# Tail of a hybrid decoder layer on one core: pools opened ahead of the attention branch, conv states moved into w_down, final norm by token quarters

## The chip, the core and the metric

One NeuronCore of a Trainium2 chip. TensorE (PE) multiplies, VectorE (DVE), ScalarE (ACT) and GpSimd (POOL) do the elementwise work, SyncE (SP) issues transfers; ACT and POOL can issue transfers on queues of their own. Each engine runs its instructions in order. The metric is the time of one execution on the device in microseconds (us).

## What is computed

One step of a one-layer decoder trunk on 1024 prompt tokens and 8 x 4 sample tokens, 1056 columns in all, in float32:

```
x      (1024 prompt + 32 sample tokens) x 1024
attn   = dilated sliding-window attention      -> 256 channels
ssm    = diagonal state space, GELU, half-GLU  -> 512 channels
mix    = sigmoid(ga) * (attn @ w_branch_attn) + sigmoid(gs) * (ssm @ w_branch_ssm)
x      = x + mix @ w_out
g, v   = halves of rmsnorm(x) @ w_up           (2816 channels each)
h      = v * silu(causal width-3 convolution of g over the tokens)
x      = x + h @ w_down
y      = rmsnorm(x)                            outputs y_prompt, y_sample
conv_p, conv_s = the last two values of g of every sequence
```

The outputs conv_p and conv_s are the "conv states" below; the caches and state-space states that are also returned are written earlier.

## The kernel before, in words

**Layout.** Channels lie on partitions (1024 = 8 chunks of 128, 2816 = 22), tokens along the free axis: 1056 columns, either as 3 pieces of 352 or as 4 quarters of 264 (256 prompt and 8 sample columns each). A float32 product is made of three matmuls: each operand is split into a high part (a cast on ACT) and a low part (a subtraction on DVE). For weights that is `load_w`: load on SP (L156), cast (L157), subtraction (L158); for activations `split` (L187, L188). The order of the instructions on each engine is mostly set by a scheduler ahead of time, from the dependences and from when the buffers of the pools come free; program text sets it only roughly.

**From the branches to w_out.** The state-space branch leaves its gated product in DRAM (`msd`), the gate logits lie there too (`sgd`). Then x is turned: x_sample is loaded (L1283), blocks are transposed on PE and copied by ACT (L1299), and eight stores on SP (L1302) keep the result in DRAM as `xtd`, to be added after w_out. The attention branch runs over 8 row groups m and 3 column pieces, 24 chunks of 128 x 352 (L1320 to L1335): the gate is loaded into a `ck` buffer on SP (L1328), sigmoid on ACT (L1329), `msd` loaded on ACT's queue (L1331), multiplied with the product on DVE (L1332), added on POOL (L1333), and split into `mh`, `ml` (L187, L188). The pool `ck` has 6 buffers of each name. After the loop the pools `low`, which hold x, are closed, and `wb` (the pool of weights for w_out, w_up and the hidden loads) is opened. w_out (L176) takes all 8 `mh`, `ml` as its k; its first result is added to `xtd` by DVE (L1374).

**w_up** (`up(f)`, 22 blocks). Seven products a block, combined by DVE; ACT, DVE and POOL make the convolution (POOL's copies L1475 to L1477, ACT L1479, DVE L1480 and L1481), silu (ACT L1482), the gain (POOL L1483) and the product `gt` (DVE L1484), and SP stores it as rows of `hd` in DRAM (L1485). `cso` keeps the last columns of each sequence.

**Conv states** (L1490 to L1499). Six times: four transposes of `cso` on PE (L145), a copy on ACT into a `gt` buffer (L1496), four small stores on SP (L1498, L1499); 24 stores in all, of 1 to 16 KB.

**w_down and the final norm.** Four quarters q of 264 columns. `hidden(q)` loads the quarter's 22 row groups from `hd` in 11 pieces (L1519) and splits them. For each of 4 pairs of output rows m there are 6 weight tiles of up to 512 KB through `load_w`, 24 matmuls to a full tile (L1560), and DVE adds the residual `y` (L1563). `turned_half` transposes half of a 128-token block (4 matmuls, L145, and an ACT copy, L1534). `norm_out` does the final norm of one block: a square with its sum over 1024 columns on ACT (L1539), the reciprocal root in small steps (L250 to L256), one multiply over 1024 columns on DVE (L1541) and the store on SP (L1542). The 32 sample tokens are collected in `sy` and normed after the loop, in a buffer from the same pool as the others.

The order of the last lines is:

```
for q in range(S4):
    ...                       # w_down, turned halves
    for b in range(2):
        norm_out(2 * q + b, yT[b], P, ypv[q, b])
    G_.tensor_copy(sy[...], y[:, :, 256:])
    hs_ = nxt
ys = fb.tile(...)             # sample tokens
for q2 in range(2):
    turned_half(ys, q2, 32, lambda k: sy[:, k])
norm_out(8, ys, 32, O[1])
```

Of the kernel before, what the change touches and what calls it, by code (L numbers as in the profile page):

```python
# [18 lines left out]
P = 128  # L19
D = 1024  # L20
NB = 8
S4 = 4
C = 264
T = S4 * C
CH = 352
NCH = 3
KD = D // P
DFF = 2816
NF = DFF // P
# [70 lines left out]
def body(tc, I, O):  # L100
    nc = tc.nc
# [11 lines left out]
    with root:  # L113
# [29 lines left out]
        def tr(out, in_):  # L143
            n = in_.shape[0]
            PE.transpose(out, in_, ident[:n, :n])  # L145
# [1170 lines left out]
        for k in range(2):  # L1316
            split(ah[k], al[k], attnF[k])
        keep.close()
        psum(8)
        ck = pool("ck", 6, stack=s6a, side="right")  # L1320
        for m in range(KD):
            if m % 4 == 0:
                w = load_w(I['w_branch_attn'][0][:, m * P:(m + 4) * P], 2, mw=4 * P)
            ps = gbanks()
            gemm(ps, w, list(zip(ah, al)), m0=m % 4 * P)
            for c in range(NCH):
                t = ck.tile([P, CH], F32, name="ck")
                nc.sync.dma_start(t, sgd[0, m * P:(m + 1) * P, cs(c)])  # L1328
                A_.activation(t, t, AF.Sigmoid)  # L1329
                t2 = ck.tile([P, CH], F32, name="ck2")  # L1330
                nc.scalar.dma_start(t2, msd[m * P:(m + 1) * P, cs(c)])  # L1331
                V_.tensor_tensor(t, ps[c][:, :CH], t, OP.mult)  # L1332
                G_.tensor_tensor(t, t, t2, OP.add)  # L1333
                split(mh[m][:, cs(c)], ml[m][:, cs(c)], t)
        s6a.close()  # L1335
        low.close()

        NK = KD // 2  # L1340
        rb1 = pool("rbp", 1).tile([P, T], F32, name="rb1")
        xa = pool("xa", 1)
        wb = pool("wo", 2)
        XO = [None] * NK
        s6y = root.enter_context(ExitStack())
        yt_ = pool("yt", 1, stack=s6y)
# [49 lines left out]
        pu_ = pool("pu", 3, PSUM, stack=s7)  # L1396
        pe_ = pool("pe", 2, PSUM, stack=s7)

        cso = ff.tile([P, NF, 18], F32, name="cso")
        n9 = ff.tile([P, 3, 9], F32, name="n9")  # L1400
        blk9 = [(j, j * P, min(P, T - j * P)) for j in range(9)]
        pt = pe_.tile([P, 512], F32, name="pe")
# [34 lines left out]
        def up(f):  # L1437
# [44 lines left out]
            A_.activation(cv, cv, AF.Silu)  # L1482
            G_.tensor_tensor(cv, cv, rb2, OP.mult)  # L1483
            V_.tensor_tensor(gt, gt, cv, OP.mult)  # L1484
            nc.sync.dma_start(hd[f * P:(f + 1) * P], gt)  # L1485

        for f in range(NF):
            up(f)

        for f0 in range(0, NF, 4):  # L1490
            n = min(4, NF - f0)
            pt = pe_.tile([P, 512], F32, name="pe")
            for f in range(n):
                tr(pt[:18, f * P:(f + 1) * P], cso[:, f0 + f])
            co_ = ff.tile([P, T], F32, name="gt", bufs=2)[:18, :512]
            A_.copy(co_[:, :n * P], pt[:18, :n * P])  # L1496
            for i in range(2):
                nc.sync.dma_start(O[7][0, :, i, f0 * P:(f0 + n) * P], co_[9 * i:9 * i + 1, :n * P])  # L1498
                nc.sync.dma_start(O[13][0, :, i, f0 * P:(f0 + n) * P], co_[9 * i + 1:9 * i + 9, :n * P])  # L1499
        s7.close()  # L1500


# [27 lines left out]
        def turned_half(yT, q2, rows, cols):  # L1530
            pt = pt_.tile([P, 512], F32, name="pt")[:rows]
            for k in range(4):
                tr(pt[:, k * P:(k + 1) * P], cols(4 * q2 + k))
            A_.copy(yT[:, q2 * 512:(q2 + 1) * 512], pt)  # L1534

        def norm_out(b, yT, rows, dst):
            f = fr[:rows, b]
            yo = wb.tile([P, KD, P], F32, name="wlo").rearrange("p k m -> p (k m)")[:rows]
            A_.activation(yo, yT, AF.Square, accum_out=f[:, 0:1])  # L1539
            rsqrt(f[:, 1:2], f[:, 0:1], f[:, 2:3], V_)  # L1540
            V_.scalar_tensor_tensor(yo, yT, f[:, 1:2], gf[:rows], OP.mult, OP.mult)  # L1541
            nc.sync.dma_start(dst, yo)  # L1542

        hs_ = hidden(0)
        for q in range(S4):
            y = fb.tile([P, KD, C], F32, name="y")
            nc.sync.dma_start(y, yd2[:, q * C:(q + 1) * C].rearrange("(m p) c -> p m c", p=P))
            nxt = None
            yT = [wb.tile([P, KD, P], F32, name="whi").rearrange("p k m -> p (k m)") for _ in range(2)]
            for m in range(0, KD, 2):  # L1550
                ps = [pg.tile([P, 512], F32, name="pd") for _ in range(2)]
                for k0 in range(0, NF, 4):
# [8 lines left out]
                                          start=k0 + k == 0 and j == 0, stop=k0 + k == NF - 1 and j == 2)  # L1561
                for x in range(2):
                    V_.tensor_tensor(y[:, m + x], ps[x][:, :C], y[:, m + x], OP.add)  # L1563
                if m == 0 and q + 1 < S4:
                    nxt = hidden(q + 1)
                if m % 4 == 2:
                    for b in range(2):
                        turned_half(yT[b], m // 4, P, lambda k, b=b: y[:, k, b * P:(b + 1) * P])
            for b in range(2):
                norm_out(2 * q + b, yT[b], P, ypv[q, b])  # L1570
            G_.tensor_copy(sy.rearrange("p k (b s) -> p k b s", s=S4)[:, :, :, q], y[:, :, 256:])  # L1571
            hs_ = nxt
        ys = fb.tile([P, KD, C], F32, name="y").rearrange("p k c -> p (k c)")[:32, :D]
        for q2 in range(2):
            turned_half(ys, q2, 32, lambda k: sy[:, k])
        norm_out(8, ys, 32, O[1].rearrange("b t d -> (b t) d"))
        s9.close()


# [31 lines left out]
```

## Time and profile before

| | |
|---|---|
| three timed runs | 1714.08, 1715.98 (median), 1721.87 us |
| the profiled execution | 1716.02 us |
| its span in the profile | 1714.2 us |
| mean granted clock of TensorE | 0.967 |
| busy share of PE, DVE, ACT, POOL | 92%, 60%, 36%, 24% |
| data moved | 234.49 MB, 137 GB/s over the span |

The span begins with the first instruction that the profile shows and ends with the last; 1.8 us lie around it. Busy times leave out the issuing of transfers and waits. In the rows below "L156" is line 156 of the kernel, an arrow reads "out <- in", and "[13.63 <-DVE wlo L158]" says how long an engine had stood idle before a row and what ended it. A name with q (SPq, ACTq) is the queue of that engine: such a row is the issue of a transfer, not its flight. "x6" means six instructions of the same kind in a row, whose times are put together.

### The profile page before, as it was taken

How to read it: one execution, taken by the hardware profiler on the slowest of the kernel's cores; microseconds unless marked ns; L12 is line 12 of the kernel's file. 1: busy time of each engine (PE TensorE's matmuls, PEld its weight loads, DVE VectorE, ACT ScalarE, POOL GpSimd, SP SyncE). 2: the span in 40 equal slices, each digit the busy share in tenths (PEclk: the TensorE clock that was granted, in tenths of full speed). 3: DMA queues.
4: the chain of work that ended last, by engine and by line, in shares of the span. 5: the costliest groups of instructions: out<-in, count | busy, mean ns of one | idle time of the engine just before them, and what ended most of it. 6: DMA issues, size and time to landing. Idle time of an engine off the chain costs nothing. (4 is left out here: it accounts for less than half of the span.)

```text
span 1714.2 us, 28810 instructions
## 1 busy us (share of the span) xinstructions
PE 1576.7 (92%) x11523; PEld 1501.0 (88%) x11523; DVE 1026.5 (60%) x1681; ACT 619.6 (36%) x1113; POOL 406.4 (24%) x419
## 2 busy tenths in 40 slices
PE   6998978999999989997699999999999957999996
PEld 5898977988888878786699999999999947999996
DVE  6546988234444434334467888888888854556453
ACT  5211221234434433325345333333333334445342
POOL 0669364022212322403221111212111110000000
PEclk9999999999999999999899999999999978999998
DMA  8263311354345436676542222222222239678552
GB/s 226 69 172 129 102 51 50 102 151 136 86 117 142 124 99 247 194 268 233 175 151 88 63 76 81 81 75 76 75 81 82 76 118 285 213 259 267 178 194 80
DMA packets 272655, 234.49 MB, mean 137 GB/s; under 512 B 33269, under 2 KB 252895, under 8 KB 272522
## 3 DMA queue, kind: packets, MB, share of 16 engines
q1 hardware_dynamic: 258842, 210.75, 40.3%
q10 hardware_dynamic: 10352, 10.38, 1.9%
q0 software_dynamic: 3328, 11.54, 1.9%
q8 instruction: 90, 1.47, 0.4%
q14 instruction: 43, 0.35, 0.1%
HBM read 184.12 MB, written 50.46 MB: 137 GB/s over the span
## 5 line engine op out<-in xcount | busy, mean ns | idle before, releaser
L158 DVE TENSOR_TENSOR wlo<-wraw,whi 128x1024 fp32r<-128x1024 f32 (+1 forms) x148 | 182.7, 1235 | 166.2 <-ACT whi L157 160.5
L176 PE MATMUL pg<-xh,wlo 128*128 128x352 f32 x816 | 213.5, 343 | 4.1 <-ACT pt__5401 L872 2.7
L157 ACT CAST whi<-wraw 128x1024 fp32r<-128x1024 f32 (+1 forms) x148 | 148.2, 1003 | 173.6 <-PE pd L1560 114.9
L176 PE MATMUL pg<-xh,whi 128*128 128x352 f32 x816 | 199.8, 326 | 0.0
L176 PE MATMUL pg<-xl,whi 128*128 128x352 f32 x816 | 199.0, 325 | 0.0
L176 PEld LDWEIGHTS pg<-xh,wlo 128*128 128x128 f32 x816 | 142.4, 191 | 15.2 <-issue 5.6
L176 PEld LDWEIGHTS pg<-xh,whi 128*128 128x128 f32 x816 | 144.7, 190 | 0.0
L176 PEld LDWEIGHTS pg<-xl,whi 128*128 128x128 f32 x816 | 144.4, 191 | 0.3
L964 POOL TENSOR_TENSOR qb<-kt,qb 128x512 f32<-128x512 f32 x48 | 65.5, 1377 | 247.7 <-DMA qb<-qd 127.7
L187 ACT CAST sh<-S 128x512 fp32r<-128x512 f32 x88 | 52.2, 619 | 77.8 <-DVE S L1451 57.1
L1571 POOL COPY sy<-y 128x64 f32<-128x64 f32 x4 | 4.0, 997 | 293.7 <-DVE y L1563 293.7
L1483 POOL TENSOR_TENSOR cv<-cv,rb 128x1056 f32<-128x1056 f32 x22 | 54.4, 2472 | 70.0 <-ACT cv L1482 70.0
L1009 ACT COPY pTs<-pT 128x256 f32<-128x256 f32 (+1 forms) x48 | 22.6, 470 | 121.1 <-PE pT L145 119.2
L188 DVE TENSOR_TENSOR sl<-S,sh 128x512 fp32r<-128x512 f32 x88 | 61.8, 704 | 0.5 <-ACT sh L187 0.5
L176 PE MATMUL pg<-mh,wlo 128*128 128x352 f32 x192 | 47.8, 330 | 13.6 <-DVE wlo L158 13.6
L1475 POOL COPY ext<-ext 128x510 f32<-128x510 f32 x22 | 13.8, 629 | 194.7 <-DVE ext L1472 194.7
L1479 ACT ACTIVATE cv<-ext,cw 128x1056 f32<-128x1056 f32 x22 | 27.9, 1270 | 79.8 <-POOL ext L1475 79.8
L176 PE MATMUL pg<-yh,wlo 128*128 128x352 f32 x144 | 48.8, 349 | 6.8 <-ACT go L473 4.2
L1466 DVE TENSOR_TENSOR ext<-ext,rb 128x528 f32<-128x528 f32 x22 | 48.5, 2204 | 0.7
L1450 DVE TENSOR_TENSOR S<-wraw 128x512 f32<-128x512 f32 x22 | 15.2, 691 | 55.9 <-DMA wraw<-in_w_up_dram 55.9
L176 PE MATMUL pg<-ml,whi 128*128 128x352 f32 x192 | 47.4, 328 | 0.0
L176 PE MATMUL pg<-mh,whi 128*128 128x352 f32 x192 | 47.1, 326 | 0.0
(1039 smaller groups left out, 4975.0 us busy)
## 6 DMA issues: line engine op xcount, KB each, us to landing
wraw<-in_w_down_dram SPq DMA_DIRECT2D x80, 512.0 KB
wraw<-in_w_up_dram SPq DMA_DIRECT2D x44, 512.0 KB
wraw<-in_w_in_dram SPq DMA_DIRECT2D x38, 512.0 KB
qb<-qd SPq DMA_DIRECT2D x48, 256.0 KB
hd<-gt SPq DMA_DIRECT2D x22, 528.0 KB
wraw<-hd SPq DMA_DIRECT2D x44, 264.0 KB
sgd<-go SPq DMA_DIRECT2D x16, 528.0 KB
kt<-in_cache_kv_w_dram SPq DMA_DIRECT2D x32, 256.0 KB
```

The lines of the kernel that those rows point to most:

```text
L157: A_.copy(hi, raw)
L158: E2.tensor_tensor(lo, raw, hi.bitcast(F32), OP.subtract)
L176: PE.matmul(ps[c][:, :CH], wt[:, k0 + k, m0:m0 + P], xt[:, c * CH:(c + 1) * CH], start=k == 0 and j == 0, stop=k == n - 1 and j == 2)
L187: A_.copy(hi, src)
L188: V_.tensor_tensor(lo, src, hi.bitcast(F32), OP.subtract)
L964: G_.tensor_tensor(qb, kv_, qb, OP.mult)
L1009: A_.copy(pTs[:, :2 * n * P], pT[:, :2 * n * P])
L1450: V_.tensor_tensor(S1, g[:, :NK], g[:, NK:], OP.add)
L1466: V_.tensor_tensor(e[:, 2:4], e[:, 2:4], h2(rb2[:, H1]), OP.mult)
L1475: G_.tensor_copy(e[:, 0:2, 1:256], e[:, 4:6, 0:255])
L1479: A_.activation(cv, ef[:, 0:T], AF.Identity, bias=cw[:, 3, f:f + 1], scale=cw[:, 0, f:f + 1])
L1483: G_.tensor_tensor(cv, cv, rb2, OP.mult)
```

## The change

1. `low` is closed ahead of the attention branch's loop, and the pools `rbp` and `wo` (`wb`) are opened there; w_branch_attn is loaded through `wb`; `ck` has 12 buffers of each name in place of 6.
2. The store of `gt` to `hd` goes out on POOL's queue in place of SP's.
3. The conv states are made by `conv_state` inside w_down's first quarter, after its first pair of rows; they use the PSUM pool `pt`, buffers named `wlo` of `wb`, and ACT's queue for the stores. `cso` lies in the pool `rbp`.
4. The final norm: the squares are summed for each half of the columns as soon as it is turned (`squares`); POOL multiplies the first half with the gain; `finish` makes the reciprocal roots of a quarter's blocks together, then ACT scales the first half and DVE multiplies the second. The sample block is turned, squared and finished inside the last quarter, in a buffer of its own; `sy` is copied for each row group.

```diff
         keep.close()
+        low.close()
         psum(8)
-        ck = pool("ck", 6, stack=s6a, side="right")
+        rbp = pool("rbp", 1)
+        wb = pool("wo", 2)
+        ck = pool("ck", 12, stack=s6a, side="right")
         for m in range(KD):
             if m % 4 == 0:
-                w = load_w(I['w_branch_attn'][0][:, m * P:(m + 4) * P], 2, mw=4 * P)
+                w = load_w(I['w_branch_attn'][0][:, m * P:(m + 4) * P], 2, mw=4 * P, pw=wb)
...
         s6a.close()
-        low.close()
...
-        rb1 = pool("rbp", 1).tile([P, T], F32, name="rb1")
+        rb1 = rbp.tile([P, T], F32, name="rb1")
+        cso = rbp.tile([P, NF, 18], F32, name="cso")
         xa = pool("xa", 1)
-        wb = pool("wo", 2)
...
-            nc.sync.dma_start(hd[f * P:(f + 1) * P], gt)
+            nc.gpsimd.dma_start(hd[f * P:(f + 1) * P], gt)
...
+        def conv_state(f0):
+            n = min(4, NF - f0)
+            pt = pt_.tile([P, 512], F32, name="pt")
+            for f in range(n):
+                tr(pt[:18, f * P:(f + 1) * P], cso[:, f0 + f])
+            co_ = wb.tile([P, KD, P], F32, name="wlo").rearrange("p k m -> p (k m)")[:18, :512]
+            A_.copy(co_[:, :n * P], pt[:18, :n * P])
+            for i in range(2):
+                nc.scalar.dma_start(O[7][0, :, i, f0 * P:(f0 + n) * P], co_[9 * i:9 * i + 1, :n * P])
+                nc.scalar.dma_start(O[13][0, :, i, f0 * P:(f0 + n) * P], co_[9 * i + 1:9 * i + 9, :n * P])
+
+        def squares(f, yT, yo, q2, rows):
+            hq = slice(q2 * 512, (q2 + 1) * 512)
+            A_.activation(yo[:rows, 512:], yT[:rows, hq], AF.Square, accum_out=f[:rows, q2:q2 + 1])
+            if q2 == 0:
+                G_.tensor_tensor(yo[:rows, hq], yT[:rows, hq], gf[:rows, hq], OP.mult)
+
+        def finish(group):
+            b0, n = group[0][0], len(group)
+            f = fr[:, b0:b0 + n]
+            V_.tensor_tensor(f[:, :, 2], f[:, :, 0], f[:, :, 1], OP.add)
+            rsqrt(f[:, :, 3], f[:, :, 2], f[:, :, 4], V_)
+            for b, yT, yo, rows, dst in group:
+                r = fr[:rows, b, 3:4]
+                A_.activation(yo[:rows, :512], yo[:rows, :512], AF.Copy, scale=r)
+                V_.scalar_tensor_tensor(yo[:rows, 512:], yT[:rows, 512:], r, gf[:rows, 512:], OP.mult, OP.mult)
+                nc.sync.dma_start(dst, yo[:rows])
...
+                if q == 0 and m == 0:
+                    for f0 in range(0, NF, 4):
+                        conv_state(f0)
...
                 if m % 4 == 2:
                     for b in range(2):
-                        turned_half(yT[b], m // 4, P, lambda k, b=b: y[:, k, b * P:(b + 1) * P])
-            for b in range(2):
-                norm_out(2 * q + b, yT[b], P, ypv[q, b])
...
+                        turned_half(ts_[b][0], m // 4, P, lambda k, b=b: y[:, k, b * P:(b + 1) * P])
+                        squares(fr[:, 2 * q + b], *ts_[b], m // 4, P)
+                    if last:
...
+                        turned_half(tS[0], m // 4, 32, lambda k: sy[:, k])
+                        squares(fr[:, 8], *tS, m // 4, 32)
+            group = [(2 * q + b, *ts_[b], P, ypv[q, b]) for b in range(2)]
+            if last:
+                group.append((8, *tS, 32, O[1].rearrange("b t d -> (b t) d")))
+            finish(group)
```

What the two programs issue, engine by engine, differs most at three places. First SP, between the state-space branch and w_out (a row that begins with - is of the kernel before, one with + of the changed one; `go` is a buffer of the state-space branch, then of x_sample; `wraw` is a weight or a hidden piece as loaded).

```order
-L1328 DMA ck<-sgd 128x352 x6
+L1275 DMA go<-sgd 128x1056 x7
 L1283 DMA go<-in_x_sample_dram 32x1024
+L156 DMA wraw<-in_w_branch_attn_dram 128x2x512 x2
+L156 DMA wraw<-in_w_out_dram 128x8x128 x2
 L1302 DMA xtd<-xl_7610 128x1056 x2
 L1302 DMA xtd<-xl_7611 128x1056 x2
 L1302 DMA xtd<-xl_7612 128x1056 x2
 L1302 DMA xtd<-xl_7613 128x1056 x2
-L1328 DMA ck<-sgd 128x352 x18
+L1331 DMA ck<-sgd 128x352 x24
```

All gate loads now stand behind the x stores, two w_out tiles ahead of them; the two w_branch_attn tiles, which had been between the `go` loads, stand behind x_sample.

Second SP, from the last hidden store to w_down. Before:

```order
L1485 DMA hd<-gt 128x1056
L1499 DMA out_dram<-gt 8x512
L1519 DMA wraw<-hd 128x2x264 x2
L1498 DMA out_dram<-gt 1x512
L1499 DMA out_dram<-gt 8x512
...
L1519 DMA wraw<-hd 128x2x264 x2
L1547 DMA y<-yd_8218 128x8x264
L156 DMA wraw<-in_w_down_dram 128x4x256 x4
```

and in the changed kernel, the whole of that stretch:

```order
L1443 DMA wraw<-in_w_up_dram 128x8x128 x42
L1509 DMA wraw<-hd 128x2x264 x11
L1563 DMA y<-yd_8219 128x8x264
L156 DMA wraw<-in_w_down_dram 128x4x256 x4
L1509 DMA wraw<-hd 128x2x264 x2
L1563 DMA y<-yd_8219 128x8x264
```

No store is left on SP here; the last of the eleven hidden loads waits for the last store of POOL's queue.

Third ACT in the changed kernel, from the last block of w_up to the first weight cast of w_down (`wlo` is the buffer of a conv state).

```order
L1480 ACTIVATE cv<-ext_9136,cw 128x1056
L1532 COPY wlo<-pt 18x512 x2
L1534 DMA out_dram<-wlo 1x512
L1535 DMA out_dram<-wlo 8x512
L1534 DMA out_dram<-wlo 1x512
L1535 DMA out_dram<-wlo 8x512
L1483 ACTIVATE cv<-cv 128x1056
...
L1532 COPY wlo<-pt 18x256
L1534 DMA out_dram<-wlo 1x256
L1535 DMA out_dram<-wlo 8x256
L157 CAST whi<-wraw 128x1024
```

The first two conv-state copies and four stores come ahead of the last silu (L1483 here), the sixth copy ahead of the first weight cast; before, one copy stood between L1479 and the silu, and no store.

## Rows read from the trace of the kernel before

**Rows 1.** The page's first part: busy time, share of the span, instructions.
```profile
PE 1576.7 (92%) x11523; PEld 1501.0 (88%) x11523; DVE 1026.5 (60%) x1681; ACT 619.6 (36%) x1113; POOL 406.4 (24%) x419
```
**Rows 2.** TensorE's waits, 690 to 950 us: total, times, longest.
```profile
PE pg L176 <- DVE wlo L158: 13.6, 1, 13.6
PE pa L145 <- DMA go<-in_x_sample_dram: 5.5, 1, 5.5
```
**Rows 3.** TensorE's waits, 1360 us to the end.
```profile
PE pd L1560 <- DVE wlo L158: 20.9, 4, 16.8
PE pe L145 <- ACT gt L1496: 12.8, 4, 6.5
```
**Rows 4.** The chain that ended last, around w_down's start: start, length, what.
```profile
1401.35 4.09 DMA hd<-gt
...
1412.92 8.34 DMA wraw<-in_w_down_dram
...
1423.64 5.66 PE pd L1560 x24
```
**Rows 5.** Timeline of SP's queue, 1406 to 1413 us.
```profile
1406.46 0.26 SPq L1498 DMA_DIRECT2D out_dram<-gt  x1
...
1411.16 0.90 SPq L1519 DMA_DIRECT2D wraw<-hd  x2
1412.15 0.41 SPq L1547 DMA_DIRECT2D y<-yd  x1
```
**Rows 6.** The chain that ended last, its end.
```profile
1704.27 2.70 DMA out_dram<-wlo
1707.08 1.16 ACT wlo L1539 x2
1709.57 1.27 DVE wlo L1541
```
**Rows 7.** One line: 256 KB stores on POOL's queue (ns to issue, us to landing).
```profile
L696 POOL DMA_DIRECT2D rtd<-r x8: 581/581/775, 125.3 to 176.3; - x8
...
DMA to landing us min/median/max: 2.3/2.4/5.5
```
**Rows 8.** Timeline of ACT, 1394 to 1398 us.
```profile
1394.98 0.57 ACT L1496 COPY gt<-pe 18x512 f32<-18x512 f32 x1 [1.33 <-DMA out_dram<-gt]
1396.40 1.08 ACT L1482 ACTIVATE cv<-cv 128x1056 f32<-128x1056 f32 x1 [0.84 <-DVE cv L1481]
```
**Rows 9.** The page's groups: busy, mean ns, idle time before and what ended it.
```profile
L1475 POOL COPY ext<-ext 128x510 f32<-128x510 f32 x22 | 13.8, 629 | 194.7 <-DVE ext L1472 194.7
```
**Rows 10.** Timeline of SP's queue, 797 to 823 us.
```profile
797.12 25.49 SPq L1328 DMA_DIRECT2D ck<-sgd  x18
822.70 0.39 SPq L156 DMA_DIRECT2D wraw<-in_w_out_dram  x1
```
**Rows 11.** Timeline of ACT in the branch loop (chunks 5, 6 and 23).
```profile
803.86 0.48 ACT L187 CAST mh<-ck 128x352 fp32r<-128x352 f32 x1 [2.93 <-DMA xtd<-xl]
...
806.55 0.49 ACT L187 CAST mh<-ck 128x352 fp32r<-128x352 f32 x1 [0.70 <-POOL ck L1333]
...
828.41 0.48 ACT L187 CAST mh<-ck 128x352 fp32r<-128x352 f32 x1 [0.68 <-POOL ck L1333]
```
**Rows 12.** Windows: PE, PEld, DVE, ACT, POOL busy; granted clock, DMA share, GB/s.
```profile
800.00:820.00 20.00, 14.61 (x82) 12.61 (x80) 13.07 (x24) 11.30 (x25) 13.11 (x12) 1.00 0.89 273
820.00:840.00 20.00, 8.85 (x42) 8.85 (x43) 10.35 (x16) 7.62 (x16) 7.42 (x7) 0.66 0.80 244
```
**Rows 13.** Groups by line, 803 to 830 us: POOL's addition.
```profile
L1333 POOL TENSOR_TENSOR ck<-ck,ck 128x352 f32<-128x352 f32 x18 | 20.5, 1165 | 9.0 <-DVE ck L1332 8.9
```
**Rows 14.** Timeline of PE at w_out's start: matmuls 1, 16 and 64.
```profile
831.15 0.66 PE L176 MATMUL pg<-mh,wlo 128*128 128x352 f32 x1 [13.63 <-DVE wlo L158]
...
835.72 0.66 PE L176 MATMUL pg<-mh,whi 128*128 128x352 f32 x3
...
843.47 0.33 PE L176 MATMUL pg<-mh,wlo 128*128 128x352 f32 x1
```

More of the change, by code (lines that the diff above doesn't have):

```diff
@@ L1397, in body @@
         pe_ = pool("pe", 2, PSUM, stack=s7)
-        cso = ff.tile([P, NF, 18], F32, name="cso")
         n9 = ff.tile([P, 3, 9], F32, name="n9")
@@ L1484, in up @@
             V_.tensor_tensor(gt, gt, cv, OP.mult)
-            nc.sync.dma_start(hd[f * P:(f + 1) * P], gt)
+            nc.gpsimd.dma_start(hd[f * P:(f + 1) * P], gt)
         for f in range(NF):
             up(f)
[L1490 to L1499, printed above, removed]
         s7.close()
@@ L1533, in turned_half, with row_tile @@
                 tr(pt[:, k * P:(k + 1) * P], cols(4 * q2 + k))
[L1534 to L1542, printed above, removed]
+            A_.copy(yT[:rows, q2 * 512:(q2 + 1) * 512], pt)
+        def conv_state(f0):
[23 more added lines that the diff above has]
+                nc.sync.dma_start(dst, yo[:rows])
+        def row_tile(name):
+            return wb.tile([P, KD, P], F32, name=name).rearrange("p k m -> p (k m)")
+        G_.memset(fr, 1.0)
         hs_ = hidden(0)
@@ L1548, in body @@
             nxt = None
-            yT = [wb.tile([P, KD, P], F32, name="whi").rearrange("p k m -> p (k m)") for _ in range(2)]
+            last = q == S4 - 1
+            ts_ = [(row_tile("whi"), row_tile("wlo")) for _ in range(2)] if q else None
             for m in range(0, KD, 2):
@@ L1563, in body @@
                     V_.tensor_tensor(y[:, m + x], ps[x][:, :C], y[:, m + x], OP.add)
-                if m == 0 and q + 1 < S4:
+                    G_.tensor_copy(sy[:, m + x].rearrange("p (b s) -> p b s", s=S4)[:, :, q], y[:, m + x, 256:])
+                if m == 0 and not last:
                     nxt = hidden(q + 1)
+                if q == 0 and m == 0:
+                    for f0 in range(0, NF, 4):
+                        conv_state(f0)
+                    ts_ = [(row_tile("whi"), row_tile("wlo")) for _ in range(2)]
                 if m % 4 == 2:
                     for b in range(2):
-                        turned_half(yT[b], m // 4, P, lambda k, b=b: y[:, k, b * P:(b + 1) * P])
-            for b in range(2):
-                norm_out(2 * q + b, yT[b], P, ypv[q, b])
-            G_.tensor_copy(sy.rearrange("p k (b s) -> p k b s", s=S4)[:, :, :, q], y[:, :, 256:])
+                        turned_half(ts_[b][0], m // 4, P, lambda k, b=b: y[:, k, b * P:(b + 1) * P])
+                        squares(fr[:, 2 * q + b], *ts_[b], m // 4, P)
+                    if last:
+                        if m == 2:
+                            both = fb.tile([P, KD, C], F32, name="y").rearrange("p k c -> p (k c)")
+                            tS = (both[:, :D], both[:, D:2 * D])
+                        turned_half(tS[0], m // 4, 32, lambda k: sy[:, k])
[4 more added lines that the diff above has]
+            finish(group)
             hs_ = nxt
[L1573 to L1576, printed above, removed]
         s9.close()
```

## The prediction

> **What bounds the kernel now.** I began with the page: TensorE is busy 92% of a span of 1714.2 us [rows 1], so a change can only win where TensorE stands still, or where something runs on after its last product. The profiled run took 1716.02 us, span plus 1.8; the three timed runs have their median at 1715.98, so both bases agree to 0.1 us. Then the list of TensorE's waits, over the two stretches that the diff touches. From 690 to 950 us there is one of 13.6 us on a weight's low part and one of 5.5 on the load of x_sample [rows 2]; from 1360 to the end 20.9 us in four waits on weights, the longest 16.8, and 12.8 us of transposes waiting for conv-state copies [rows 3]. The 12.8 lie between the last w_up product and the first w_down product, so by themselves they delay nothing. Third, the chain of work that ended last, for what stands behind the 16.8 us [rows 4]; fourth, SP's rows there [rows 5]; last, the tail, where TensorE has no more to do [rows 6].
>
> **1. Start of w_down.** The chain reads: the last hidden store leaves at 1401.35 and lands 4.09 us later (1405.4); the first w_down tile is issued at 1412.92 and is there after 8.34 (1421.3); the first product starts at 1423.64, 2.4 later, cast and subtraction [rows 4]. What fills SP from 1405.4 to 1412.9 are two hd loads, 12 of the 24 small conv-state stores, two more hd loads that waited for their buffers, and y [rows 5]. After the change SP has there one hd load, y and w_down: the small stores are on ScalarE's queue and the hidden store on GpSimd's. The store still waits for the same VectorE product (about 1401.0; its issue costs GpSimd 0.58 us by the 256 KB stores that it issues elsewhere [rows 7]), so it lands near 1405.4 again. Then SP issues one hd load (0.45, half of a pair) and y (0.41) [rows 5]: w_down at 1406.4, **6.5 us** earlier. I keep 8.34 for its flight, since y goes ahead in both, and the 2.4 behind it. TensorE starts at 1417.2 in place of 1423.6: gain 6.4.
>
> Bounds: the unknown is the landing of a 528 KB store from GpSimd's queue. The nearest rows, 256 KB, land after 2.3 to 5.5 us [rows 7]; against 4.09 that is 1.8 better to 1.4 worse, and the size may add 1. The flight of the weight may fall by 1, with fewer hd loads beside it. So 4 to 9. I stay at 4.09, which is a store of this very size. On ScalarE the change puts a moved copy (0.57) and four issues (SP's price 0.26 each [rows 5]), 1.6 us, ahead of the last silu; ScalarE was idle there for 1.33 and 0.84 us [rows 8], so they fit with 0.6 to spare, and if they did not, the store would be late by the excess. The first weight cast stands behind the sixth copy, whose buffer waits for stores issued before 1405, well ahead of 1415.
>
> The page "DMA: Bandwidth & Descriptors" of the Trainium skill ("Anatomy of one DMA — SWDGE (gpsimd) path") gives about 2.0 us plus bytes/436e3 for such a transfer: an estimate by it of 3.2 us for 528 KB, by which the sum would be 0.9 us better. The trace's 4.09 for the same bytes, from the other queue, stays in the sum.
>
> **2. The w_up loop: nothing.** 22 stores of 0.58 us [rows 7] move to GpSimd, which waits 194.7 us in all, 8.9 us a time, ahead of the copy that follows each in its queue [rows 9]. Without that cover each would delay the copy, and the convolution behind it, by 0.58 us: 13 us at most.
>
> **3. Branch to w_out.** The 13.6 us [rows 2] go back to the loop over 24 chunks: the w_out weight is loaded behind the ck loads, at 822.70 [rows 10], and cast after the last chunk's cast at 828.41 [rows 11]; the product starts at 831.15 [rows 14]. In the change the two first w_out tiles are loaded ahead of the x stores, and cast after chunk 17 on ScalarE, so the product can start six chunks before the loop ends; its last two row groups (k = 6 and 7) then meet the loop's end. Against that, all 24 ck loads now stand behind the x stores and wait for their landing; before, six had gone ahead and 18 followed at 797.12 [rows 10]. The last x store landed at about 803.5 (ScalarE's cast at 803.86 had waited for it [rows 11]). SP's queue ahead of x_sample loses six ck loads and two branch weights, and gains two w_out tiles and those same branch weights behind it; I take the landing at 800 to 803.5. The first cast comes 5 us later: 2.5 for a load (the wait of 2.93 in [rows 11] as the price), 0.5 sigmoid, 0.5 multiply, 1.17 GpSimd's addition [rows 13]. The pace was (828.41 - 806.55)/17 = 1.29 us a chunk [rows 11], just over GpSimd's 1.165 [rows 13]; by traffic, 360 KB a chunk at 244 to 273 GB/s [rows 12] give 1.32 to 1.48. With 1.17 to 1.48, chunk 17 is cast at 825 to 834 and the product starts 2.4 later, at 827 to 836, middle 831: the start alone gains nothing sure. But with less idle time before it the first products should run at the full clock. From 831.15 to 835.72 there are 15 in 4.57 us, while the next 48 take 7.75, 0.16 each [rows 14]; the granted clock from 820 to 840 is 0.66 [rows 12]. 15 x 0.16 is 2.4, so 2.1 us are to be had. I put the place at **2 us gained**; a start at 836 makes it -3, one at 827 with the full clock +6.
>
> **4. Within w_down.** The three shorter waits, 20.9 - 16.8 = 4.1 us [rows 3], lie at the quarter ends, where two 1024-wide multiplies (1.27 each, as in the tail [rows 6]) stand ahead of a weight's low part on VectorE. The change makes them 512 wide and gives the other half to ScalarE and GpSimd; the sums of squares come per half. I expect 1 of the 4.1 back. But the hd loads of the second quarter now alternate one to one with w_down tiles, and a cast that waits for one holds up the weight cast behind it. No row prices this; the waits at hand may go or double: -4 to +4.
>
> **5. The tail.** Before: the chain ends with a store that is awaited for 2.70 us, since the sample block needs its buffer, then its squares at 1707.08, its multiply at 1709.57 (1.27), and 3.4 us to the end of the span [rows 6]. After: half of each block is turned and squared earlier, and the sample block has a buffer of its own. Once its last transposes are there (about 1697.8) ScalarE has three copies of 0.57 [rows 8] and three squares of 512 (half of 1.16 [rows 6]), 3.5 us and 0.5 for the sums' reads: 1701.8. One root and the small VectorE steps for all three blocks, 1.4 by what lies from 1708.2 to 1709.6 here; then three half-width multiplies on each of two engines, 0.64 each, 1.9: 1705.1; and 3.4 for the last store: 1708.5, **5.7 us** less. I take 5, as three stores of 1.1 MB now leave together. Bounds 3.5 to 6.5.
>
> **Sum:** 6.4 + 0 + 2 + 1 + 5 = 14.4; 1716.0 - 14.4 = 1701.6, put down as **1701.5**. The terms' bounds (4 to 9, -3 to 6, -4 to 4, 3.5 to 6.5), taken as independent, spread it by some 6 us either way.
>
> **Rivals.**
> *The branch stage loses.* The ck stream is bound by traffic at 1.48 us a chunk and begins at 803.5: the product starts at 836, 5 later, less 2 of clock: -3 in place of +2, and with no gain at the quarter ends 1707.5. For it: a DMA share of 0.80 to 0.89 there [rows 12]. Against: 1.29 was the pace that the same traffic allowed. Chance 0.17.
> *The branch stage closes up.* The product starts at 827 at the full clock: +6 or 7, 1697. For it: its weights are there some 40 us ahead. Chance 0.12.
> *The hidden store on GpSimd lands late.* While VectorE works on SBUF the store's start is held; its landing stretches as the 256 KB ones did, from 2.3 to 5.5 [rows 7], 3.2 us: 1704.7. Chance 0.1. The page "SBUF — State Buffer" of the Trainium skill ("SBUF: two separate sides") warns of just this move: a DMA from GpSimd's queue is held while VectorE is in a two-port mode, 3100 ns in place of 620. By it the start of w_down would lose another 2.5 us. That median and minimum are 0.1 apart in [rows 7] speaks against its being common here.
> *Slower: GpSimd paces w_up.* If the issue held GpSimd past its idle time ahead of the copy, 8.9 us [rows 9], ScalarE and VectorE would be late and TensorE run out of free PSUM in every block. To be slower than 1724.6 each of the 22 must lose (1724.6 - 1701.5)/22 = 1.05, an issue of 9.9 us; at 10.2 it is 1730. For it: no row shows a 528 KB store from this queue. Against: 0.58 us [rows 7]. Chance 0.04.
> *The change does not take hold.* Something else on SP, say a wait shared with ScalarE's small stores, keeps w_down's load at 1412.9. The sum without 6.4: 1708. Chance 0.07.
>
> **How the numbers follow.** A measurement of this kernel can tell about 0.5%, 8.6 us, from no change: faster is below 1707.4, slower above 1724.6. My forecast has 0.5 (1697 to 1706), closing up 0.12, the late store 0.1, the branch loss 0.17 (half on either side of 1707.4), no hold 0.07, paced 0.04. Faster: 0.5 + 0.12 + 0.1 + 0.08 and a little of the rest, 0.82; slower 0.03; same 0.15. The range leaves out the paced case and the ends of the others: 1693 to 1709.5.
>
> **What would show it.** Right: the wait at the first w_down product near 10 us, its weight issued near 1406; in the tail no wait on a store, and the last multiply about 8 us after the last product; the first w_out products 0.16 us apart, and the 13.6 down to about 10. Wrong: a first ck load landing after 806, ck loads ending most of ScalarE's waits in the branch loop; new waits on hd loads in w_down's first quarter; GpSimd's copy L1475 starting late in w_up.

## The result, and the profile after

The changed kernel took 1692.86 us in the median of four runs (1688.57 to 1698.85), the kernel before 1717.12 in the runs made beside it: a ratio of 0.9859, 95% interval 0.9817 to 0.9900. That is faster, by less than 2% but clear of the spread, and 0.14 us below the lower end of the range. Timed again beside the kernel before in more rounds (the first run of the second group below) the ratio was 0.989, interval 0.9874 to 0.9907: 18.8 us, 16 to 21.5, against a forecast of 14.4. The size below is taken from there and from the profiles.

I cut both profiled executions at the same places of the program: the first gate load of the state-space branch, w_out's first product, w_up's first and last product, w_down's first and last product.

| stage, us | before | after | difference |
|---|---|---|---|
| start to the first gate load | 699.1 | 700.9 | +1.8 |
| gate load to w_out's first product | 132.1 | 133.0 | +0.9 |
| w_out, to w_up's first product | 96.0 | 95.4 | -0.6 |
| w_up, 22 blocks | 462.9 | 458.6 | -4.3 |
| gap, to w_down's first product | 33.6 | 25.7 | -7.9 |
| w_down | 273.2 | 267.8 | -5.5 |
| tail, to the end of the span | 17.3 | 12.5 | -4.9 |
| span | 1714.2 | 1693.8 | -20.4 |

**The branch stage.** TensorE's waits of the changed kernel from 690 to 930 us (total, times, longest):

```profile
PE pg L176 <- DVE ck L1335: 10.7, 2, 9.5
PE pg L176 <- DVE wlo L158: 6.1, 1, 6.1
...
PE pa L145 <- DMA go<-in_x_sample_dram: 1.6, 1, 1.6
```

The 13.6 us of [rows 2] are 6.1, and the 5.5 are 1.6; but the wait on the chunks' multiplies, 2.8 us in the kernel before, is 10.7. SP's timeline and its waits from 770 to 835 us, and ScalarE's timeline, say why (start, length):

```profile
788.49 8.71 SPq L1302 DMA_DIRECT2D xtd<-xl  x8
804.27 22.49 SPq L1331 DMA_DIRECT2D ck<-sgd  x24
```

```profile
SPq L1331 <- DMA xtd<-xl: 6.9, 2, 5.3
```

```profile
806.73 0.50 ACT L1332 ACTIVATE ck<-ck 128x352 f32<-128x352 f32 x1 [15.43 <-DMA ck<-sgd]
...
808.83 0.49 ACT L187 CAST mh<-ck 128x352 fp32r<-128x352 f32 x1 [1.21 <-POOL ck L1336]
...
830.40 0.48 ACT L187 CAST mh<-ck 128x352 fp32r<-128x352 f32 x1 [0.29 <-POOL ck L1336]
...
831.19 1.97 ACT L157 CAST whi<-wraw 128x1024 fp32r<-128x1024 f32 x2
```

All 24 gate loads wait until the x stores have landed, at 804.27. ScalarE, which in the kernel before cast its sixth chunk at 803.86 [rows 11], casts its first at 808.83. Chunk 17 and the weights behind it come when the whole loop used to be done, and the first products, from 833.85, are again at half speed (1.2 in place of 2.4 GHz), 0.29 us apart in place of 0.16:

```profile
833.85 0.66 PE L176 MATMUL pg<-mh,wlo 128*128 128x352 f32 x1 [6.11 <-DVE wlo L158]
834.31 0.49 PE L176 MATMUL pg<-ml,whi 128*128 128x352 f32 x1
```

**The gap.** TensorE's waits from 1385 us to the end, POOL's last store, SP's queue, and the chain:

```profile
PE pd L1577 <- DVE wlo L158: 18.9, 3, 18.0
PE pt L145 <- DVE gt L1474: 3.9, 1, 3.9
```

```profile
1400.34 0.59 POOL L1486 DMA_DIRECT2D hd<-gt  x1 [1.59 <-DVE gt L1485]
```

```profile
1403.70 0.36 SPq L1509 DMA_DIRECT2D wraw<-hd  x1
1404.22 0.36 SPq L1563 DMA_DIRECT2D y<-yd  x1
1404.69 5.42 SPq L156 DMA_DIRECT2D wraw<-in_w_down_dram  x4
```

```profile
1404.69 6.51 DMA wraw<-in_w_down_dram
1411.22 1.05 ACT whi L157
1412.30 1.24 DVE wlo L158
1413.58 21.34 PE pd L1577 x156
```

From the last w_up product, leg by leg, before (from [rows 4]) and after: to the last store 11.3 and 12.5; the store's landing 4.1 and 3.4; from there to the issue of w_down's tile 7.5 and 1.0; its flight 8.3 and 6.5; to the product 2.4 and 2.4. The 1.2 lost at first are the conv-state copies and stores, which ScalarE has ahead of the last silu and which waited for transposes (the 3.9 us). In second profiles of the two kernels (below) that leg is 11.6 and 11.7, so most of the 1.2 belongs to this execution.

**The tail** has no wait on a store any more. Its chain, which answers to [rows 6], from the squares to the last multiply:

```profile
1683.77 1.23 ACT wlo L1540 x4
1685.01 0.62 ACT y L1540 x2
...
1687.31 0.75 DVE wlo L1553
1688.06 0.66 DVEq L1633
1688.72 0.65 DVE y L1553
```

The last multiply ends at 1689.4, 8.0 us after the last product.

### The profile page after: what moved, and what is told of

Its sections match the earlier page's. It is cut to its first block, busy times and chain, and to the rows that moved or that the text cites. A ratio compares the mean times of both kernels' runs of the same rounds, so it can differ in the third digit from the quotient of the medians.

```text
span 1693.8 us, 28884 instructions
## 1 busy us (share of the span) xinstructions
PE 1576.6 (93%) x11523; PEld 1501.7 (89%) x11523; DVE 1020.9 (60%) x1655; ACT 625.1 (37%) x1135; POOL 462.7 (27%) x479
## 5 line engine op out<-in xcount | busy, mean ns | idle before, releaser
L964 POOL TENSOR_TENSOR qb<-kt,qb 128x512 f32<-128x512 f32 x48 | 65.9, 1385 | 245.4 <-DMA qb<-qd 163.0
L1581 POOL COPY sy<-y 128x8 f32<-128x8 f32 x32 | 31.5, 983 | 226.0 <-DVE y L1580 225.4
L176 PE MATMUL pg<-yl,whi 128*128 128x352 f32 x144 | 46.5, 333 | 0.0
L176 PE MATMUL pg<-yh,whi 128*128 128x352 f32 x144 | 46.4, 335 | 0.0
```

The costliest lines, as they stand in the source:

```text
L176: PE.matmul(ps[c][:, :CH], wt[:, k0 + k, m0:m0 + P], xt[:, c * CH:(c + 1) * CH], start=k == 0 and j == 0, stop=k == n - 1 and j == 2)
L964: G_.tensor_tensor(qb, kv_, qb, OP.mult)
L1581: G_.tensor_copy(sy[:, m + x].rearrange("p (b s) -> p b s", s=S4)[:, :, q], y[:, m + x, 256:])
```

## The experiments

Sixteen kernels in four groups; in a group all ran on one chip beside the kernel before. The interval of each ratio is 95%, and a ratio always stands to the kernel before.

### One part of the change undone

**The final norm as before**, `norm_out` with its 1024-wide square and multiply, and the sample block after the loop:

```diff
-            finish(group)
+            for b in range(2):
+                norm_out(2 * q + b, yT[b], P, ypv[q, b])
```

> The changed kernel with the final norm of the kernel before. Theory (each part pays in its own stage): the tail goes from 12.45 back to about 17.3 us and w_down from 267.8 back to about 271 to 273, since the 1024-wide multiplies stand before weights at the quarter ends again; the gap between w_up and w_down stays at 25.7. Some 8 to 10 us slower than the changed kernel. Rival (w_down became shorter because hidden loads alternate with weight tiles, or because of the conv states' move): w_down stays at 268, only the tail's 4.9 us come back.

Measured: ratio 0.9956 (0.9939 to 0.9972), some 11 us slower than the changed kernel (0.989 in the repeat), a little more than I had said. The tail is 17.4 us, w_down 270.6, the gap 25.3. The quarter ends are back:

```profile
PE pd L1561 <- DVE wlo L158: 21.9, 3, 17.2
```

21.9 - 17.2 = 4.7 us in two waits, against 0.9 in the changed kernel. The norm pays in the tail and at the quarter ends.

**The conv states as before**, at the end of w_up, on SP's queue:

```diff
-                    for f0 in range(0, NF, 4):
-                        conv_state(f0)
...
+        for f0 in range(0, NF, 4):
+            n = min(4, NF - f0)
+            pt = pe_.tile([P, 512], F32, name="pe")
...
+            co_ = ff.tile([P, T], F32, name="gt", bufs=2)[:18, :512]
```

> The changed kernel with the conv states back at the end of w_up, their stores on SP and their buffers those of gt. Theory: the gap between the last w_up product and the first w_down product goes from 25.7 back to 32 to 34 us, for the small stores stand ahead of w_down's tiles on SP; w_down 267 to 269 and the tail 12.5 as in the changed kernel. 6 to 8 us slower. Rival (the hidden store on GpSimd's queue brought the gap's gain): the gap stays at 26 to 28.

Measured: 0.9947 (0.9928 to 0.9966); gap 30.9, w_down 266.9, tail 12.5. Two misses: the gap is shorter than the 32 to 34 expected, and the kernel is some 10 us slower than the changed one, not 6 to 8. Five of the gap's eight us are the conv states'.

**The hidden store on SP's queue:**

```diff
-            nc.gpsimd.dma_start(hd[f * P:(f + 1) * P], gt)
+            nc.sync.dma_start(hd[f * P:(f + 1) * P], gt)
```

> The changed kernel with the hidden stores on SP's queue again. Theory: the stores are off the path, so w_up's 458.6 us came from the execution and not from the change: w_up anywhere from 458 to 463, and the gap within 1 us of 25.7 (SP's issue is 0.2 shorter, the landing 4.1 in place of 3.4). Within 3 us of the changed kernel. Rival (SP was held by the stores in w_up, and the weights of w_up came late): w_up goes back to 463, with stalls of DVE L1464 and L1467 in two blocks, and 4 us are lost.

Measured: 0.9924 (0.9909 to 0.9938); w_up 459.0, gap 28.2. The rival falls: w_up keeps its length without the store's move. But the gap is 2.5 us longer, which I had put within 1, and the kernel some 6 us slower than the changed one, not within 3. The store lands 4.6 us after its issue (1397.34 to 1401.92) in place of 3.4, and w_down's tile, issued at 1403.01, is cast only here:

```profile
1411.35 1.04 ACT L157 CAST whi<-wraw 128x1024 fp32r<-128x1024 f32 x1 [5.42 <-DMA out_dram<-wlo]
```

The wait is put down to a conv-state store that stands ahead on ScalarE's queue.

**The branch pools as before:**

```diff
-        low.close()
         psum(8)
-        rbp = pool("rbp", 1)
-        wb = pool("wo", 2)
-        ck = pool("ck", 12, stack=s6a, side="right")
+        ck = pool("ck", 6, stack=s6a, side="right")
```

> The changed kernel with the pools of the attention branch as before (ck of 6 buffers, low closed after the loop, w_branch_attn through the old pool). Theory (the place gains nothing, since the ck stream waits for the x stores): from the first gate load of the state-space branch to w_out's first product 132 us as in the kernel before, against 133.0; w_out 96.0 against 95.4; the total within 1 us of the changed kernel. Rival (the earlier w_out weights pay, and the profile of the changed kernel fell on a bad phase): 2 to 4 us slower than the changed kernel.

Measured: 0.9918 (0.9897 to 0.9940), which overlaps the changed kernel's 0.9874 to 0.9907; the middles are some 5 us apart, where I had said within 1 and the rival 2 to 4. From the last product of the state-space branch to w_out's first it takes 61.4 us, in the changed kernel 60.0, in the kernel before 59.9; the gap is 24.9. In the branch stage no difference stands out of the spread. w_up is 463.2 here, the longest of all profiles; the account of the prediction comes back to it.

### The changed kernel again, and two waits taken away

**Nothing altered.**

> The changed kernel, nothing altered, timed again beside the kernel before in more rounds. Theory (its profile's stages tell the whole gain: gap 7.9, w_down 5.5, tail 4.9 and, from w_up, 4.3 that come and go with the execution): a ratio of 0.988 to 0.991, 15 to 20 us. Rival (the 24 us of the first medians are the gain): a ratio of 0.985 to 0.987. Its w_up is 458 to 463 us long if that length comes and goes, 458.6 again if it belongs to the change.

Measured: 0.989 (0.9874 to 0.9907). Stages: w_up 460.6, gap 24.9, w_down 269.1, tail 12.5. The first medians overstated the gain; w_up was not 458.6 again.

**Six gate buffers:**

```diff
-        ck = pool("ck", 12, stack=s6a, side="right")
+        ck = pool("ck", 6, stack=s6a, side="right")
```

> The changed kernel with 6 buffers of each name in the pool ck in place of 12, so that the gate loads no longer wait for the x stores; pools and w_out's early loads stay. Theory (the branch stage gains nothing in the change because the first cast of a chunk moved from 793.5 to 808.8, and chunk 17 with it): the first six chunks run ahead of the x stores again, chunk 17 is cast 6 to 8 us earlier, and from the last product of the state-space branch to w_out's first product it takes 53 to 57 us in place of 60. 3 to 7 us faster than the changed kernel. Rival (the place is bound by GpSimd's additions or by traffic whatever the order): 59 to 61 us, no gain.

Measured: 0.9826 (0.9809 to 0.9844), 1680.5 us. From the last product of the state-space branch to w_out's first: 50.2 us, in the run beside it 59.1. TensorE's waits from 690 to 935:

```profile
PE pa L145 <- DMA go<-in_x_sample_dram: 6.5, 1, 6.5
PE pg L176 <- DVE ck L1335: 4.2, 2, 3.6
```

No wait on a w_out weight is left. The first w_out product starts at 819.30, and in the window that follows (PE, PEld, DVE, ACT, POOL busy; granted clock, DMA share, GB/s) the clock is full:

```profile
820.00:840.00 20.00, 20.00 (x127) 20.00 (x126) 14.62 (x21) 9.41 (x19) 8.54 (x8) 1.00 0.65 221
```

The first chunk's cast and the casts of the two w_out tiles on ScalarE:

```profile
793.70 0.49 ACT L187 CAST mh<-ck 128x352 fp32r<-128x352 f32 x1 [2.91 <-POOL ck L1336]
...
804.31 1.04 ACT L157 CAST whi<-wraw 128x1024 fp32r<-128x1024 f32 x1
...
820.04 1.05 ACT L157 CAST whi<-wraw 128x1024 fp32r<-128x1024 f32 x1
```

The wait for the x stores is what held the stage. One step differs from the expectation: chunk 17 is cast at 824.18, 6.2 us earlier, as expected, but the first w_out tile was cast at 804.31, right behind the sixth chunk, so the product starts ahead of chunk 17. The stage's 8.9 us are on the path: the median is 11.6 us below the changed kernel's beside it, more than I had said (3 to 7). Another 2.2 come from w_out, 93.4 us in place of 95.6, without the half-speed start.

**w_down's weights first:** the last hidden piece on GpSimd's queue, and two buffers for the weights' parts.

```diff
-        w2 = pool("w2", 3, stack=s9, side="right")
+        w2 = pool("w2", 2, stack=s9, side="right")
...
-                nc.sync.dma_start(h2(r), hd[...])
+                (nc.gpsimd if q == 0 and j == NH - 1 else nc.sync).dma_start(h2(r), hd[...])
```

> The changed kernel with the last of the first quarter's hidden loads on GpSimd's queue, behind the store that it waits for, and two in place of three buffers for the high and low parts of w_down's weights (so that their pool lies in memory that TensorE alone had been reading). SP then has no wait for the last hidden store ahead of w_down's first tile. Theory (the gap that is left, 25.7 us, is the chain from the last store over SP to the weight, and none of it is needed by the first product): the first w_down tile is issued within 2 us of the last w_up product, the gap falls to 10 to 14 us; two buffers cost 0 to 4 us in w_down. 8 to 15 us faster than the changed kernel. Rival (the first product waits for the last hidden piece or the conv-state copies anyway): the gap stays above 20 us.

Measured: 1.000 (0.9985 to 1.0014), 18.7 us slower than the changed kernel. The gap fell to 8.0 us, further than forecast. But w_down takes 301.3 us: the third buffer is worth some 32 us (the next group has it alone), not 0 to 4.

**Both together:**

> The edits of the two kernels before this one together: ck of 6, the last hidden load on GpSimd's queue, two buffers for w_down's weight parts. Theory: the gains add, 11 to 20 us faster than the changed kernel, a ratio of 0.977 to 0.984 to the kernel before. Rival: what is saved early comes back as waits later, and it is within 5 us of the changed kernel.

Measured: 0.9923 (0.9906 to 0.9940). Branch 50.4 us, gap 8.6, w_down 299.4: the parts add, the price of the third buffer too, so that it is 5.6 us slower than the changed kernel and not 11 to 20 faster.

### What the third buffer costs, and w_down's start without giving it up

**Two buffers alone:** the first half of the diff before the last.

> The changed kernel with two in place of three buffers for the high and low parts of w_down's weights, and nothing else. Theory (the kernel with the weights first lost its gain of 17 us in the gap to the third buffer alone): the gap stays near 25 us and w_down takes 299 to 303 us in place of 268, some 32 us slower than the changed kernel, more than the kernel before. Rival (the hidden load on GpSimd's queue or the early weights upset w_down's order): w_down stays below 280 us.

Measured: 0.9999 (0.9983 to 1.0015); w_down 299.6, as expected. The gap I got wrong: it is 8.7 us here too, with the hidden load still on SP. So what held the weights was not the queue of the hidden load but their third buffer: with two, SP issues the first tiles from 1385.15, 0.8 us ahead of the end of the last w_up product. My reading of the program is that the pool reaches into the place of `gt` with three buffers, so that its first load must wait for the last hidden store, and with two does not; no run here has three buffers and nothing but the hidden load moved. TensorE's waits from 1365 us:

```profile
PE pd L1577 <- DVE wlo L158: 22.0, 24, 4.9
```

The stalls are many and short: 22.0 us in 24.

**Eight gate buffers:** `pool("ck", 8, ...)`.

> The changed kernel with 8 buffers of each name in the pool ck. Theory (what counts is that the first gate loads lie clear of the x stores; the number after that matters little): eight loads go ahead of the x stores, from the last product of the state-space branch to w_out's first product 48 to 52 us, as with six (50.2), within 3 us of that kernel and 9 to 14 faster than the changed one. Rival (more in flight is better): below 47 us.

Measured: 0.9851 (0.9828 to 0.9874), branch 51.9 us. All eight first gate loads are issued by 776.3, the x stores from 794.45. Clear of the x stores is what counts; eight are no better than six.

**Weights first with three buffers:** six gate buffers; the last hidden piece and the first `y` on GpSimd's queue, written after three of the first weight tiles; and in `up`

```diff
+            gt = ff.tile([P, T], F32, name="gt", bufs=2)
+            cv = ff.tile([P, T], F32, name="cv")
             r1, u2, u3, u4 = (h2(ff.tile([P, HALF], F32, name=n)) for n in ("r1", "u2", "u3", "u4"))
-            gt = ff.tile([P, T], F32, name="gt", bufs=2)
...
-            cv = ff.tile([P, T], F32, name="cv")
```

> The kernel with ck of 6, and w_down's weights ahead of the last hidden store without giving up the third buffer: the last hidden piece and the first y are loaded on GpSimd's queue and written later in the program, and gt and cv take their places first in w_up's pool, so that the weights' pool lies over tiles that VectorE has read by the last w_up product. Theory: the first cast stands behind the fifth conv-state copy on ScalarE and not behind the last hidden load, the gap is 16 to 19 us in place of 25.9, w_down 267 to 270; 7 to 9 us faster than with ck of 6 alone, a ratio of 0.977 to 0.979 to the kernel before. Rival (the first tile's wait is only moved to the second tile, whose cast stands behind the last hidden piece): the gap falls and w_down grows by as much.

Measured: 0.9796 (0.9771 to 0.9821), 1674.45 us: the fastest of all kernels here, though its interval meets that of six gate buffers alone. The gap is 21.3, w_down 268.4. The gap fell by 4.6 us and not by 7 to 9. The chain that ended last shows what stood ahead of the weight:

```profile
1383.42 3.70 DMA rb<-in_norm_f_g_dram
...
1387.20 0.37 SPq L156
```

w_down's first tile was released by the landing of the final norm's gain, which has nothing to do with it.

**The same with eight gate buffers:**

> The same with ck of 8. Theory: within 3 us of the kernel with 6. Rival (more gate loads ahead pay): 3 us or more faster.

Measured: 0.9828 (0.9805 to 0.9851): gap 19.7, w_down 269.6, branch 52.5. It is 5 us slower than with six, where I had said within 3; the intervals meet. Not better than with six.

### The parts alone, on the kernel before

**The kernel before again:**

> The kernel before, nothing altered, with a profile of its own. Theory (w_up's length comes and goes with the execution: TensorE's clock in the first block, single stalls in two others): w_up is 458 to 463 us long and need not be 462.9 again; the gap 33 to 34, w_down 272 to 274, the tail 17.3. Rival (the pools of the kernel before cost w_up 3 us): 462.5 to 463.5, as in the kernel with the old branch pools (463.2).

Measured: 1.001 (0.9996 to 1.0023); w_up 460.5, gap 33.8, w_down 271.6, tail 17.3. So w_up's 462.9 was in part the execution's. The changed kernel's second profile had 460.6, but with a longer stretch at half speed; how much of the difference is left at the same clock is worked out below.

**The new norm alone:**

> The kernel before with the new final norm alone. Theory: the tail is 12.5 and the stalls of w_down at the quarter ends fall from 4.1 us to under 2, w_down 268 to 270 in place of 273; the gap stays 33.6. 7 to 10 us faster than the kernel before, a ratio of 0.994 to 0.996. Rival (the quarter ends came free through the hidden loads' new order): w_down 271 to 273, 5 us, 0.997.

Measured: 0.9947 (0.9931 to 0.9964), 9.1 us. Tail 12.6, w_down 266.5, gap 34.6. One stall of 0.4 us is left in w_down:

```profile
PE pd L1576 <- DVE wlo L158: 17.5, 2, 17.1
```

The norm alone clears the quarter ends; conv states and hidden loads are as before in this kernel.

**The new branch pools alone:**

> The kernel before with the attention branch's new pools alone (ck of 12). Theory: nothing, within 3 us of the kernel before, with 59 to 62 us from the last product of the state-space branch to w_out's first product. Rival (the pools shorten w_up through where the weights lie): 3 to 5 us faster, w_up 458 to 460.

Measured: 0.9987 (0.9974 to 1.0000), 2.2 us, and none at the interval's end; 60.0 us from product to product, w_up 461.1. The branch stage gains nothing.

**The gain's load later:** weights first with three buffers, and the load of `gf` written after `conv_state`.

> The kernel with ck of 6 and the weights first under three buffers, with the load of the final norm's gain written after the conv states. Theory (w_down's first load stood for 14 us behind that gain's load, whose semaphore it shares): it is issued 3 to 8 us after the last w_up product, and the first cast then waits on ScalarE for the last conv-state copy alone: gap 17 to 22 against 21.3, up to 4 us faster. Rival (the copies on ScalarE, not the weight, set the gap): 20 to 22 us, no gain.

Measured: 0.9814 (0.9789 to 0.9839): gap 20.1, no gain that can be told from the kernel that it was to mend. w_down's first tile is issued at 1386.38, still 11.8 us after the last product, so the expected issue was a miss. SP's waits from 1372 to 1408 us show what stands ahead of it now, a conv-state store in the place of the gain's load:

```profile
SPq L156 <- DMA out_dram<-wlo: 17.6, 4, 12.4
```

The tile is issued 0.85 us before the last hidden store is (1387.23), so with `gt` in another place it does not wait for that store. Its cast, at 1392.29, stands right behind the last conv-state copy (1391.62), as the rival had it; whether the weight was there earlier the profile does not tell.

## Why the prediction was right or wrong

**Start of w_down (6.4, bounds 4 to 9): 7.9, and 8.7 in the second profile.** The mechanism is as forecast: SP's leg from landing to issue went from 7.5 us to 1.0, the 6.5 of the prediction. Two legs were mis-sized: the flight, kept at 8.34, is 6.5; and the store from GpSimd's queue lands in 3.4, not 4.09. Over all 22 stores (issue in ns, landing in us):

```profile
L1486 POOL DMA_DIRECT2D hd<-gt x22: 595/595/612, 980.7 to 1400.3; - x22
...
DMA to landing us min/median/max: 3.0/3.0/3.9
```

The Trainium skill ("DMA: Bandwidth & Descriptors", "Anatomy of one DMA — SWDGE (gpsimd) path") gives 2.0 us plus bytes/436e3, an estimate of 3.2 for this size. These rows, 3.0, agree with it. The 4.09 that I kept was the landing of one store among other transfers, not the price of the size.

The Trainium skill ("SBUF — State Buffer", "SBUF: two separate sides") has a DMA from GpSimd held while VectorE is in a two-port mode. None of the 22 took longer than 3.9 us; whether VectorE was in such a mode then, no run shows. In other profiles the median is 3.0 too, with single stores of up to 5.3.

That the copies and stores on ScalarE fit ahead of the last silu failed in the first profile (1.2 us lost) and held in the second (0.1). Undone one at a time, conv states and hidden store cost 5.1 and 2.5 us of gap, together close to the whole.

**w_up (0): about 2.** Of the 4.3 us between the first two profiles 1.7 are clock. w_up's first block has a stretch at half speed, 6.8 us long in the kernel before and 3.4 in the changed one; windows of that block, before and after (the number ahead of the DMA share is the granted clock):

```profile
935.00:940.00 5.00, 4.48 (x20) 4.48 (x21) 5.00 (x9) 4.98 (x9) 0.52 (x3) 0.50 0.34 101
940.00:945.00 5.00, 5.00 (x37) 5.00 (x36) 4.03 (x8) 0.55 (x1) 0.00 (x0) 0.85 0.35 105
```

```profile
937.00:942.00 5.00, 4.41 (x25) 4.41 (x26) 5.00 (x9) 4.98 (x9) 0.59 (x3) 0.66 0.36 106
942.00:947.00 5.00, 5.00 (x44) 5.00 (x43) 4.86 (x10) 0.62 (x1) 0.00 (x0) 1.00 0.36 105
```

Over all eighteen profiles w_up lies between 458.6 and 463.2, and that stretch is 3.4, 6.8 or 10.2 us long. Set side by side at the same length, the four profiles with the old branch pools are the longer ones each time: 460.5 against 458.6; 462.9 against 458.9 to 460.5; 462.2 and 463.2 against 460.6 to 461.7. The four average 462.2, the fourteen with the new pools 460.2. So about 2 us of the gain come with the pools opened ahead of the branch, and not with the store: w_up is 459.0 with the store back on SP. This was seen in profiles made for other ends, and the pools alone were timed at 2.2 us (none to 4.4), so the size is uncertain. The step of the prediction that failed is that it put w_up at nothing by looking at GpSimd's queue alone; what about the pools shortens w_up, no run here shows.

**Branch to w_out (+2, -3 to +6): 0.** The bounds held, the point did not. The stage is 0.9 us longer, w_out 0.6 shorter. The step that failed is the clock: I had the start at 831 and the first products at full speed, "with less idle time before it". The start is at 833.9, and 6.1 us of idle time were enough: half speed again. The rival of the branch stage that loses had the right mechanism, gate loads behind the x stores; its -3 was too dark, and traffic was not its cause: ScalarE's casts wait for GpSimd's additions, nine of which run from 812.25 in 10.43 us, without a wait between them. Chunk 0 was cast at 808.8, where I had 805 to 808.5, and chunk 17 at 830.4, in the middle of my 825 to 834. The 2.5 us for a gate load were right by luck: the 2.93 of [rows 11] that I took as the price is a wait for an x store, while the load took 2.46 (issued at 804.27, its sigmoid at 806.73). That the place holds 10 us if the loads are not held back, six gate buffers showed.

**Within w_down (+1, -4 to +4): about 3.6.** The term that missed by most. Two parts, both of the norm. The stalls at the quarter ends fell from 4.1 us to 0.9 (1.9 in the second profile), where I had given back only 1 of the 4; the new waits on hidden loads that I feared did not come. The rest of the 5.5 in the first pair of profiles is clock: products run slowly at w_down's start and behind a stall, for 9.4 us in the kernel before and 4.7 in the changed one, which at half speed is 2.3 us. The granted clock of the first 8 us, in the kernel before and after:

```profile
1423.60:1431.60 8.00, 7.96 (x43) 7.96 (x44) 3.65 (x4) 3.41 (x5) 0.00 (x0) 0.62 1.09 353
```

```profile
1413.60:1421.60 8.00, 8.00 (x48) 8.00 (x49) 5.10 (x5) 3.60 (x5) 0.00 (x0) 0.70 1.09 357
```

Five products more in the second. That part varies from execution to execution: w_down took 269.6 to 273.2 in four profiles with the old norm (mean 271.2), 266.5 to 269.1 in eight with the new one and w_down's loads as in either kernel (mean 267.6). Hence 3.6.

**The tail (5): 4.9.** Right, by its own steps: 8.0 us from the last product to the last multiply, 4.4 to the end.

**Sum.** With these sizes, 7.9 to 8.7 + 2 + 0 + 3.6 + 4.9 = 18.4 to 19.2, against 18.8 (16 to 21.5) timed. The forecast had 14.4. The direction was right, and three of the four places where it saw a gain. What failed is the size of four terms: w_down (1, measured 3.6), its start (6.4, measured 7.9 and 8.7), w_up (0, measured about 2) and the branch stage (+2, measured 0). That the last two cancel is luck. The range missed the first median by 0.14 us, since its lower end allowed for 23 us and that comparison came out at 24.3. The repeat, 0.989 of 1716.0 or 1697, lies inside it.

## What to carry to other kernels

A load held by the order of its queue and a load held by the memory that it is to fill look the same in a timeline: both pools that mattered here (12 gate buffers over x, three weight buffers over `gt`) made a load wait for a store to land, the second by my reading of the program and the runs that fit it. More buffers can cost more than they bring when the added ones lie over something that is still on its way out; look for the first instruction of a pool that waits for a store. And a stage's length from one pair of profiles should be set against a second pair before it is explained: here 4.3 us of w_up shrank to about 2 once profiles of the same clock were set side by side.

## What was not expected of the hardware

A 528 KB store from GpSimd's queue landed in 3.0 us (median of 22, at most 3.9). In the chain the last such store took 4.1 and 4.6 from SP's queue in two kernels, but that does not make GpSimd's queue the faster one. By the DMA packets of the traces, the last data packet of a store ended 2.3 us after its issue from SP's queue (median of 22, kernel before) and 2.7 after its issue from GpSimd's (changed kernel); only the last store, with other transfers under way, took SP's queue 3.7 and 4.1 and GpSimd's 2.9.

TensorE's first products ran at half speed, 0.29 us apart in place of 0.16, in w_out after 6.1 us of idle time; in the kernel with six gate buffers, which does not idle there, the granted clock was 1.00.
